# Filler products moved between the slots of attention and the stage behind it in a one-layer decoder block

## The chip, the cores and the metric

The kernel runs on one core of a Trainium2 chip. The metric is the device time of one execution in microseconds (us). Before the change it is 1077.14 us, the median of three runs (1077.08 to 1079.26). The product of two float32 matrices is made of three products of split operands throughout: each operand is written as a high part (rounded to fp32r) plus a low part (the rest), and high by high, high by low and low by high are summed in PSUM. So each "product" below is one TensorE instruction of a triple.

## The reference, cut to what matters

One layer over 1024 tokens of width 1024, all float32:

```
h   = rms_norm(x, norm1_g);  z = h @ w_in                  # 1024 x 2304
mix = [pool mixer | short gated conv | conformer conv | differential attention]   # 4 x 256 columns
x   = x + mix @ w_out
h2  = rms_norm(x, norm2_g)
x   = x + (silu(h2 @ w_gate) * (h2 @ w_up)) @ w_down       # inner width 2816

attention, 4 heads, each with two score maps m = 0, 1 of depth 32:
  p_m = softmax(q_m k_m^T / sqrt(32) + relative bias, causal)
  o   = rms_norm((p_0 - lam * p_1) @ v) * (1 - lam_init)
```

## The kernel before, in words

**Stages.** First come the norm and the input projection with the three convolution mixers (to about 244 us), then attention (244 to 400 us), then the end of the output projection and the second norm (to about 450 us), then the gated feed-forward part, which makes up the rest and which the change does not touch.

**Attention** is cut into 16 units u = 4p + h (p: a pair of 128-token query tiles, h: a head). `unit` writes down, for each of the two query tiles i and the two maps m, the scores (TensorE, line 673), the bias and the row minimum (VectorE, lines 680 and 681) and the exponential (ScalarE, line 684). VectorE then joins the two maps (lines 686 to 688). For each of the p + 1 key blocks kb, TensorE transposes the joined map (line 699), ScalarE and VectorE split it into high and low parts (lines 703 and 704), and TensorE multiplies it with v (line 708), first with the high parts, then with the low ones. Every second unit ends with a transposition of the output (line 720, tile `oT`). `prep_q` makes the stacked queries of the next heads (`kst`, made by ScalarE and by POOL or VectorE, transposed at line 510).

**Fillers.** Beside that runs a queue `fillq` of TensorE work that attention does not wait for. In order it holds the 288 products of the output projection of the three other mixers (`gen_partial`: 16 tiles of 18 products, numbered 1 to 288 here, tile `fm`), then for each finished p the 25 steps of `out_attn`, and at the last p two times four steps of `norm2`. `fill1` takes the next n steps from the queue, where n is the next entry of FQ:

```
def fill1(ins, n=None):
    for _ in range(next(slots, 0) if n is None else n):
        ...
                    with tc.issue_after(ins.ins):
                        f()
```

`issue_after(ins)` lets the filler be issued on TensorE only behind `ins`, the attention instruction that was just written. The call is the gate, its place in the text is the rank. One `fm` bank in PSUM serves all tiles of `gen_partial`, so the first product of a tile waits until the bank of the tile before has been read out (line 632 on ScalarE or line 635 on VectorE). The weights of `w_out` come in two column halves c, each of three pairs of tiles (a high one by line 120 or 122, a low one by POOL at line 134). Products 1 to 144 use half 0, products 145 to 288 half 1, which is loaded into the same six buffers.

**The slots.** FQ has 180 entries, one for each call of `fill1` without a count. A unit has two slots at `prep_q` (units 4, 8 and 12 at their start for their own second half of heads; units 2, 6 and 10 for the next p), four at the scores, two for each key block (after the transposes, and after the product with the high parts), one at its end, and one after `oT` in odd units. The units begin at slots 0, 7, 15, 24, 32, 43, 53, 64, 74, 87, 99, 112, 124, 139, 153 and 166. In both kernels the queue is empty at slot 179.

**The stage behind attention.** A second queue holds 48 products of the first gate and up columns, and later 48 more. `run_fill` writes a generator's steps and takes `ns[n]` fillers behind its step n + 1. FL and FB use up 27 of the first 48, while the last `out_attn` runs. FA stands behind the four transposition steps of `norm2(PO[2])`, where 21 are left. FC stands behind those of `norm2(PO[3])`, with the second 48. `drain` writes down what is left, without gates.

**Order.** The text is not the order of execution. The framework plans it (`schedule_with_timeline_sim=True`): on each engine it takes the instruction written first among those that its own simulated clock holds ready, and the engine then runs this fixed order. An instruction that is held back by its inputs in that plan is overtaken by later ones.

Of the kernel before, what the change touches and what calls it, by code (L numbers as in the profile page):

```python
# [33 lines left out]
PQ0 = 2  # L34
PQ1 = 0
PO = [0, 1, 2, 3]
FQ = [13, 0, 1, 0, 4, 0, 0, 0, 0, 0, 5, 6, 1, 4, 0, 0, 0, 0, 6, 1, 2, 5, 1, 0, 3, 0, 0, 2, 0, 4, 0, 1, 6, 0, 1, 9, 0, 1, 0, 0, 3, 5, 0, 3, 1, 4, 0, 3, 2, 0, 0, 4, 0, 5, 2, 0, 1, 1, 0, 2, 0, 0, 0, 0, 1, 0, 2, 0, 0, 0, 7, 0, 0, 0, 0, 0, 0, 5, 5, 5, 5, 0, 2, 7, 2, 0, 0, 3, 3, 3, 3, 0, 1, 2, 0, 2, 2, 0, 0, 1, 1, 10, 0, 3, 1, 0, 3, 4, 0, 1, 0, 0, 12, 4, 2, 1, 3, 2, 8, 1, 3, 0, 2, 6, 2, 0, 1, 5, 4, 2, 2, 3, 2, 1, 2, 0, 1, 0, 0, 2, 1, 0, 0, 4, 0, 0, 1, 0, 3, 0, 1, 4, 0, 0, 0, 2, 0, 14, 6, 0, 1, 12, 2, 1, 9, 3, 0, 0, 0, 3, 1, 2, 13, 10, 0, 3, 0, 4, 0, 20]
FL = [9, 1, 2, 0, 0, 2]
N2F = 0
FA = [0, 5, 19, 17]  # L40
FB = [11, 1, 0, 0, 0, 0, 0, 0, 0, 0, 0, 0, 0, 0, 1, 0, 0, 0, 0, 0, 0, 0, 0, 0, 0]
FC = [11, 5, 5, 2]
X1 = [1, 1, 1, 1, 1, 1, 1, 1, 0, 1, 1, 1, 0, 1, 1, 1]
SPE = [2, 2, 1, 0, 0, 1, 0, 1, 1, 0, 0, 0, 0, 1, 2, 2, 0, 2, 0, 2, 0, 0, 0, 0, 0, 1, 0, 0, 0, 0, 0, 0, 1, 0, 0, 0, 2, 1, 0, 1, 2, 2, 2, 2, 2, 2, 0, 0]
WOE = [0, 0, 1, 0, 1, 0, 0, 0]
# [21 lines left out]
def tile_hybrid(ctx, tc, x, norm1_g, w_in, pool_w, pool_scale, sconv_w, conf_w, conf_b, ln_g, ln_b,  # L67
# [570 lines left out]

    slots = iter(FQ)

# [101 lines left out]
    def out_attn(p, ps_o=None):  # L742
        ps_o = ps_o or ps_fm
        if p == PO[0]:
            wo[3] = [load_wo(3, c) for c in range(2)]
        ps = ps_tp()

        def tr():
            for k in range(2):
                for i in range(2):  # L750
                    ins = T.transpose(ps[:, k * 256 + i * P:k * 256 + (i + 1) * P], qn[p][:, i, k * P:(k + 1) * P], ident)
            return ins

        yield tr
        mh = misc.tile([P, 2, 256], R, name="mh", tag="mh")
        ml = misc.tile([P, 2, 256], R, name="ml", tag="ml")
        psv = ps.rearrange("p (a b) -> p a b", a=2)
        A.activation(mh, psv, AF.Copy, scale=subg)
        V.scalar_tensor_tensor(ml, psv, subg, mh.bitcast(F), op0=ALU.mult, op1=ALU.subtract)
        for i in range(2):  # L760
            t = 2 * p + i
            for c in range(2):
                po = ps_o()
                W = wo[3][c]
                for k in range(2):
                    yield from mms(po, (mh[:, k, i * P:(i + 1) * P], ml[:, k, i * P:(i + 1) * P]), (W[0][:, k], W[1][:, k]),
                                   k == 0, k == 1)
                sl = slice(c * 512, (c + 1) * 512)
                if X1B[PO.index(p)]:
                    tm = stp.tile([P, 512], F, name="tm", tag="st")  # L770
                    A.copy(tm, po)
                    G.tensor_tensor(x1[t][:, sl], x1[t][:, sl], tm, op=ALU.add)
                else:
                    V.tensor_tensor(x1[t][:, sl], x1[t][:, sl], po, op=ALU.add)

    def drain():
        while fillq:
            f = next(fillq[0], None)
            if f is None:
                fillq.pop(0)  # L780
            else:
                f()
# [10 lines left out]
    def norm2(p, ps_n=None):  # L793
        if p == PO[0]:
            W0.append(wgu(w_gate, 0))
            h2["hi"] = [m8.tile([P, 4, 512], R, name="h2a", tag="m8"), m8.tile([P, 4, 512], R, name="h2b", tag="m8")]
            h2["lo"] = [m8.tile([P, 4, 512], R, name="h2c", tag="m8")]
            h2["lo"] += [spp.tile([P, 512], R, name=f"h2lo{k}", tag="sp") for k in range(4)]
        if p == PO[2]:
            h2["k1"] = [ktp.tile([P, 2, 4, 512], R, name=f"h2k{k}", tag="KT") for k in range(2)]  # L800
        c0 = (p % 2) * 256
        xn = norm_xn([x1[2 * p], x1[2 * p + 1]], lambda: stp.tile([P, 1024], F, name="xn2", tag="st"), split=NX[PO.index(p)])

        def diff(kt, src):
            o, d = (tf[i][:, kt % 4, c0:c0 + 256] for i in (1, 2))
            if kt < 4:
                hi, lo = (a[:, c0:c0 + 256].bitcast(F) for a in h2rhs(0, kt))
                V.scalar_tensor_tensor(o, src, g2[:, kt:kt + 1], hi, op0=ALU.mult, op1=ALU.subtract)
                V.tensor_tensor(o, o, lo, op=ALU.subtract)
            else:  # L810
                V.scalar_tensor_tensor(d, src, g2[:, kt:kt + 1], o, op0=ALU.mult, op1=ALU.subtract)

        yield from norm_T(xn, g2, lambda kt: tuple(a[:, c0:c0 + 256] for a in h2rhs(p // 2, kt)),
                          ps_n or ps_tp, 2, diff if p // 2 == 1 else None)

    def wgu(w, f0, wpool=None, tag="w", stage=None):
        return wsplit(w[:, f0:f0 + P].rearrange("(k p) c -> p k c", p=P), (8,), wpool, tag, stage)
# [28 lines left out]
    def gu_items(k, W):  # L846
        for s in range(2):
            for kt in range(8):
                yield from mms(pgu[k][s], (W[s][0][:, kt], W[s][1][:, kt]), h2rhs(PO[0] // 2, kt), kt == 0, kt == 7)

    def run_fill(gen, ns):
        for n, f in enumerate(gen):
            ins = f()
            fill1(ins, ns[n % len(ns)])

    def alt(*ts):
        n = [0]

        def nxt():
            n[0] += 1  # L860
            return ts[n[0] % len(ts)]() if callable(ts[0]) else ts[n[0] % len(ts)]

        return nxt
# [4 lines left out]
    if N2F:  # L868
        run_fill(norm2(PO[2], alt(ps_tp, ps_fm)), FA)
    run_fill(out_attn(PO[3], alt(*pgu[1])), FB)  # L870
# [7 lines left out]
    if not N2F:  # L878
        run_fill(norm2(PO[2], alt(ps_tp, ps_fm)), FA)
    W1 = [wgu(w, P, _B(ap4, b), t, ap4.tile([P, 1024], F, name="st1", tag="at", bufs=ATB))  # L880
          for w, b, t in ((w_gate, PT1, "pt1"), (w_up, PT0, "pt0"))]
    fillq.append(gu_items(1, W1))
    run_fill(norm2(PO[3], alt(ps_tp, ps_fm)), FC)
    drain()
# [301 lines left out]
```

## Time and profile before

| | us |
|---|---|
| median of three runs | 1077.14 |
| the profiled execution | 1077.97 |
| its span, first to last instruction | 1076.2 |
| TensorE busy | 1045.2 (97%) |
| VectorE busy | 736.7 (68%) |
| ScalarE busy | 439.8 (41%) |
| GpSimd (POOL) busy | 222.9 (21%) |
| mean granted TensorE clock | 0.995 |

How to read it: the engines are PE (TensorE, with PEld for its weight loads), DVE (VectorE), ACT (ScalarE), POOL (GpSimd) and SP (the queue that issues transfers). L673 is line 673 of the kernel. A matrix product is shown with its latency, so the busy time of PE overlaps itself in a dense stretch. The distance between the starts of two products tells what one costs there.

### The profile page before, as it was taken

What the parts mean: (1) busy time and instruction counts of PE and PEld (TensorE: products, weight loads), DVE (VectorE), ACT (ScalarE), POOL (GpSimd) and SP (SyncE); (2) the same over time, 40 slices, a digit from 0 to 9 for tenths busy, and PEclk for the clock granted to TensorE, in tenths of its full rate; (3) what the DMA queues carried; (4) which work ended last, traced back from release to release, by engine and by line L of the source; (5) the groups of instructions that cost most, each with busy time, mean ns of one, the idle gap of its engine ahead of it and who ended that gap; (6) DMA issues with size and microseconds to landing.
All of it is one profiled execution on the core that took longest, in us unless ns stands there. A gap on an engine that the chain in (4) does not pass through costs nothing.

```text
span 1076.2 us, 13520 instructions
## 1 busy us (share of the span) xinstructions
PE 1045.2 (97%) x5203; PEld 875.9 (81%) x5203; DVE 736.7 (68%) x1127; ACT 439.8 (41%) x710; POOL 222.9 (21%) x202
## 2 busy tenths in 40 slices
PE   7999999998989989899999999999999999999998
PEld 6878879996778877787888888888888878888886
DVE  5599995648899966886676566567657656755541
ACT  5512124536786766432432333333233343433320
POOL 5137124665675643000000000000000000000000
PEclk8999999999999999999999999999999999999999
DMA  8131110111021130022353454445255286866721
GB/s 217 49 98 40 59 40 21 40 41 40 30 79 41 49 93 25 9 61 88 117 207 101 162 206 148 131 171 200 94 176 205 101 311 230 295 196 212 233 103 40
DMA packets 89664, 128.04 MB, mean 119 GB/s; under 512 B 17112, under 2 KB 57600, under 8 KB 87040
## 3 DMA queue, kind: packets, MB, share of 16 engines
q1 hardware_dynamic: 89600, 127.18, 35.9%
q8 instruction: 41, 0.67, 0.3%
q14 instruction: 23, 0.19, 0.1%
HBM read 94.13 MB, written 33.04 MB: 118 GB/s over the span
## 4 chain that ended last, share of the span: by engine, by line
PE 81%; DVE 8%; DMA 4%; ACT 3%; issue 1%; POOL 1%; SPq 1%; ACTq 0%; POOLq 0%; DVEq 0%
PE sb L139 11%; PE sb L138 11%; PE sb L140 11%; PE mm L139 6%; PE mm L140 6%; PE mm L138 6%; PE dx L140 3%; PE dx L139 3%; PE dx L138 3%; PE dy L138 3%; PE dy L140 3%; PE dy L139 3%; PE fm L604 1%; PE fm L606 1%; PE fm L605 1%
## 5 line engine op out<-in xcount | busy, mean ns | idle before, releaser
L139 PE MATMUL sb<-T,rhi 128*128 128x512 f32 x320 | 124.6, 389 | 0.0
L140 PE MATMUL sb<-T,rlo 128*128 128x512 f32 x320 | 124.5, 389 | 0.0
L138 PE MATMUL sb<-T,rhi 128*128 128x512 f32 x320 | 124.5, 389 | 0.0
L911 DVE TENSOR_TENSOR dq<-ds,dq 128x2048 fp32r<-128x2048 f32 x35 | 79.9, 2290 | 57.0 <-ACT dq L910 53.9
L910 ACT CAST dq<-ds 128x2048 fp32r<-128x2048 f32 x35 | 66.6, 1912 | 105.8 <-PE dy L140 34.5
L134 POOL TENSOR_TENSOR wlo<-st,whi 128x1024 fp32r<-128x1024 f32 (+2 forms) x30 | 73.9, 2468 | 109.7 <-ACT whi L120 98.5
L138 PE MATMUL mm<-hT,whi 128*128 128x512 f32 (+1 forms) x224 | 79.6, 367 | 2.6 <-ACT whi L120 2.0
L139 PE MATMUL mm<-hT,whi 128*128 128x512 f32 (+1 forms) x224 | 81.4, 367 | 0.6 <-DVE hT L200 0.5
L140 PE MATMUL mm<-hT,wlo 128*128 128x512 f32 (+1 forms) x224 | 80.6, 363 | 0.3 <-POOL wlo L134 0.3
L317 DVE SCALAR_TENSOR_TENSOR t<-u,cw,t 128x1023 f32<-128x1023 f32 (+28 forms) x58 | 71.4, 1266 | 0.7
L140 PEld LDWEIGHTS sb<-T,rlo 128*128 128x128 f32 x320 | 60.1, 188 | 12.5
L138 PEld LDWEIGHTS sb<-T,rhi 128*128 128x128 f32 x320 | 60.1, 188 | 12.5
L139 PEld LDWEIGHTS sb<-T,rhi 128*128 128x128 f32 x320 | 60.1, 188 | 12.4
L910 ACT CAST rhi<-st 128x1024 fp32r<-128x1024 f32 x28 | 29.5, 1054 | 98.4 <-PE sb L139 49.5
L139 PE MATMUL dx<-dq 128*128 128x512 f32 x160 | 62.5, 390 | 1.3 <-DVE dq L911 1.3
L140 PE MATMUL dx<-dq 128*128 128x512 f32 x160 | 62.3, 390 | 0.0
L138 PE MATMUL dx<-dq 128*128 128x512 f32 x160 | 61.3, 390 | 0.0
L684 ACT ACTIVATE pt<-sc,mx 128x128 f32<-128x128 f32 (+7 forms) x64 | 47.6, 747 | 18.2 <-DVE mx L681 18.1
L138 PE MATMUL mm<-whi,hT 128*128 128x256 f32 x192 | 55.0, 290 | 0.0
L139 PE MATMUL mm<-wlo,hT 128*128 128x256 f32 x192 | 54.7, 286 | 0.0
L140 PE MATMUL mm<-whi,hT 128*128 128x256 f32 x192 | 54.5, 285 | 0.0
L1031 DVE TENSOR_TENSOR tp<-tp,sb 128x512 f32<-128x512 f32 x30 | 20.5, 684 | 45.2 <-PE sb L140 45.2
(342 smaller groups left out, 2698.3 us busy)
## 6 DMA issues: line engine op xcount, KB each, us to landing
ds<-dL SPq DMA_DIRECT2D x35, 512.0 KB, 4.1
wd<-in_w_down_dram SPq DMA_DIRECT2D x10, 1024.0 KB, 5.2
dT<-wd SPq DMA_DIRECT2D x10, 1024.0 KB, 6.0
dL<-afs SPq DMA_DIRECT2D x10, 1024.0 KB, 3.9
ds<-dT SPq DMA_DIRECT2D x20, 512.0 KB, 6.0
st<-in_w_in_dram SPq DMA_DIRECT2D x18, 512.0 KB, 3.8
st<-in_w_gate_dram SPq DMA_DIRECT2D x15, 512.0 KB, 4.2
st<-in_w_up_dram SPq DMA_DIRECT2D x15, 512.0 KB, 3.7
```

The lines of the kernel that those rows point to most:

```text
L134: G.tensor_tensor(lo[:, nv:], st[:, nv:], hi[:, nv:].bitcast(F), op=ALU.subtract)
L138: T.matmul(ps, lhsT=L[0], rhs=Rr[0], start=first, stop=False, skip_group_check=more)
L139: T.matmul(ps, lhsT=L[0], rhs=Rr[1], start=False, stop=False, skip_group_check=more)
L140: return T.matmul(ps, lhsT=L[1], rhs=Rr[0], start=False, stop=last, skip_group_check=more)
L317: V.scalar_tensor_tensor((z if s == 30 else acc)[:, s:], u[:, :S - s], w[:, 30 - s:31 - s], acc[:, s:], op0=ALU.mult, op1=ALU.add)
L604: yield lambda: T.matmul(ps, lhsT=L[0], rhs=Rr[0], start=first, stop=False)
L605: yield lambda: T.matmul(ps, lhsT=L[0], rhs=Rr[1], start=False, stop=False)
L606: yield lambda: T.matmul(ps, lhsT=L[1], rhs=Rr[0], start=False, stop=last)
L684: A.activation(pts[m][:, 0:w], sc[:, 0:w], AF.Exp, bias=mx, scale=-1.0, accum_out=lt[:, h, m, i:i + 1])
L910: A.copy(hi, src)
L911: (eng or V).tensor_tensor(lo, src, hi.bitcast(F), op=ALU.subtract)
L1031: V.tensor_tensor(s, s, ps, op=ALU.add)
```

## The change

Three lists of quotas are changed and nothing else. The sum of FQ stays 387.

```
-FQ = [13, 0, 1, 0, 4, 0, 0, 0, 0, 0, 5, 6, 1, 4, 0, 0, 0, 0, 6, 1, 2, 5, 1, 0, 3, 0, 0, 2, 0, 4, 0, 1, 6, 0, 1, 9, 0, 1, 0, 0, 3, 5, 0, 3, 1, 4, 0, 3, 2, 0, 0, 4, 0, 5, 2, 0, 1, 1, 0, 2, 0, 0, 0, 0, 1, 0, 2, 0, 0, 0, 7, 0, 0, 0, 0, 0, 0, 5, 5, 5, 5, 0, 2, 7, 2, 0, 0, 3, 3, 3, 3, 0, 1, 2, 0, 2, 2, 0, 0, 1, 1, 10, 0, 3, 1, 0, 3, 4, 0, 1, 0, 0, 12, 4, 2, 1, 3, 2, 8, 1, 3, 0, 2, 6, 2, 0, 1, 5, 4, 2, 2, 3, 2, 1, 2, 0, 1, 0, 0, 2, 1, 0, 0, 4, 0, 0, 1, 0, 3, 0, 1, 4, 0, 0, 0, 2, 0, 14, 6, 0, 1, 12, 2, 1, 9, 3, 0, 0, 0, 3, 1, 2, 13, 10, 0, 3, 0, 4, 0, 20]
+FQ = [16, 0, 1, 3, 4, 0, 0, 0, 3, 0, 7, 6, 1, 4, 0, 0, 0, 0, 6, 1, 2, 3, 1, 0, 3, 0, 0, 3, 0, 4, 0, 1, 2, 0, 1, 5, 0, 1, 0, 0, 3, 3, 0, 3, 1, 4, 0, 3, 2, 0, 0, 4, 0, 10, 2, 0, 1, 1, 0, 2, 0, 0, 0, 0, 1, 0, 2, 0, 0, 0, 5, 0, 0, 0, 5, 0, 0, 5, 4, 4, 4, 0, 7, 3, 2, 1, 0, 2, 2, 2, 2, 0, 1, 2, 0, 2, 2, 0, 0, 1, 1, 7, 0, 3, 1, 0, 3, 4, 0, 1, 0, 0, 12, 4, 2, 1, 3, 2, 8, 1, 3, 0, 2, 6, 2, 0, 1, 5, 4, 2, 2, 3, 2, 1, 2, 0, 1, 0, 0, 2, 1, 0, 0, 4, 0, 0, 1, 0, 3, 0, 1, 4, 0, 0, 0, 2, 0, 14, 8, 0, 1, 12, 7, 1, 6, 2, 0, 0, 0, 3, 1, 2, 10, 10, 0, 3, 0, 4, 0, 20]
-FA = [0, 5, 19, 17]
+FA = [0, 11, 19, 23]
-FC = [11, 5, 5, 2]
+FC = [6, 4, 3, 2]
```

Slot by slot, with the number of fillers by which the changed queue is ahead after it ("lead"):

| slots (unit) | change | lead after |
|---|---|---|
| 0, 3 (u0), 8, 10 (u1) | +3, +3, +3, +2 | 11 |
| 21 (u2), 27 (u3) | -2, +1 | 10 |
| 32, 35, 41 (u4) | -4, -4, -2 | 0 |
| 53 (u6, first prep step) | +5 | 5 |
| 70 (u7) | -2 | 3 |
| 74 (u8, first prep step) | +5 | 8 |
| 78, 79, 80 (u8) | -1 each | 5 |
| 82, 83, 85 (u8) | +5, -4, +1 | 7 |
| 87 to 90 (u9) | -1 each | 3 |
| 101 (u10) | -3 | 0 |
| 158, 162, 164, 165 (u14) | +2, +5, -3, -1 | 3 |
| 172 (u15) | -3 | 0 |

In FA, 21 fillers are left: before, 5 and 16 are taken behind the second and the third step; now 11 and 10. In FC, 23 of 48 are gated before, 15 now.

## Rows read from the trace of the kernel before

**Rows 1.** The page: TensorE's busy line, and the chain that ended last, by engine.

```profile
PE 1045.2 (97%) x5203; PEld 875.9 (81%) x5203; DVE 736.7 (68%) x1127; ACT 439.8 (41%) x710; POOL 222.9 (21%) x202
...
PE 81%; DVE 8%; DMA 4%; ACT 3%; issue 1%; POOL 1%; SPq 1%; ACTq 0%; POOLq 0%; DVEq 0%
```

**Rows 2.** Stretches: us; busy PE, PEld, DVE, ACT, POOL (instructions); clock, DMA, GB/s.

```profile
244.00:261.00 17.00, 14.16 (x70) 10.49 (x69) 14.60 (x51) 9.12 (x34) 9.74 (x9) 1.00 0.15 48
261.00:284.00 23.00, 22.43 (x124) 17.98 (x123) 20.39 (x68) 16.81 (x47) 17.30 (x21) 1.00 0.11 35
284.00:298.00 14.00, 12.61 (x77) 10.46 (x76) 12.30 (x42) 11.02 (x30) 7.64 (x11) 1.00 0.10 33
298.00:306.00 8.00, 8.00 (x46) 6.88 (x46) 7.51 (x20) 6.01 (x14) 4.14 (x5) 1.00 0.16 54
306.00:318.00 12.00, 9.39 (x57) 7.52 (x56) 11.89 (x27) 10.34 (x23) 10.00 (x8) 1.00 0.21 67
318.00:332.00 14.00, 12.96 (x75) 10.99 (x76) 13.17 (x37) 9.51 (x22) 8.54 (x7) 1.00 0.26 89
332.00:374.00 42.00, 42.00 (x245) 36.34 (x243) 39.24 (x83) 29.74 (x59) 27.71 (x32) 1.00 0.14 45
...
434.00:446.00 12.00, 9.21 (x49) 6.97 (x48) 11.14 (x27) 7.11 (x15) 0.89 (x2) 0.98 0.00 0
```

**Rows 3.** TensorE in time order, 246 to 257 us: start, duration, [idle before <-releaser].

```profile
251.02 0.73 PE L673 MATMUL sc<-KT,QT 128*128 128x256 f32 x2 [0.69 <-ACT pt L684]
...
256.34 0.44 PE L699 MATMUL tp<-ident,pt 128*128 128x128 f32 x2 [0.51 <-DVE pt L688]
```

**Rows 4.** TensorE and VectorE in time order about slots 32 to 35.

```profile
272.21 0.48 PE L606 MATMUL fm<-whi,sp 128*128 128x512 f32 x1
...
275.07 0.39 PE L606 MATMUL fm<-whi,sp 128*128 128x512 f32 x1
...
275.96 0.27 PE L699 MATMUL tp<-ident,pt 128*128 128x128 f32 x1
...
274.35 1.16 DVE L688 SCALAR_TENSOR_TENSOR pt<-pt,cf 128x512 f32<-128x512 f32 x1
```

**Rows 5.** TensorE in time order: four waits, and the filler behind the last.

```profile
292.05 0.66 PE L510 MATMUL tp<-ident,kst 128*128 128x128 f32 x4 [1.14 <-POOL kst L506]
...
314.01 0.74 PE L708 MATMUL av<-at,VV 128*128 128x256 f32 x4 [1.19 <-DVE at L704]
...
324.73 0.50 PE L605 MATMUL fm<-wlo,sp 128*128 128x512 f32 x1 [0.93 <-POOL wlo L134]
...
387.79 0.51 PE L708 MATMUL av<-at,VV 128*128 128x256 f32 x2 [1.27 <-DVE at L704]
...
388.38 0.48 PE L604 MATMUL fm<-whi,mh 128*128 128x512 f32 x1
```

**Rows 6.** TensorE 303 to 309 us, and the ScalarE copy that the transposes at L720 read.

```profile
303.05 0.39 PE L604 MATMUL fm<-whi,sp 128*128 128x512 f32 x1
...
305.34 0.39 PE L605 MATMUL fm<-wlo,sp 128*128 128x512 f32 x1
305.57 0.60 PE L720 MATMUL tp<-ident,oT 128*128 128x128 f32 x4
306.01 0.60 PE L510 MATMUL tp<-ident,kst 128*128 128x128 f32 x4
...
308.39 0.66 PE L510 MATMUL tp<-ident,kst 128*128 128x128 f32 x4 [1.08 <-POOL kst L506]
...
302.84 0.59 ACT L120 COPY oT<-av 128x512 f32<-128x512 f32 x1 [0.29 <-PE av L708]
```

**Rows 7.** POOL: the addition for the last tile of half 0, and the third low part of half 1.

```profile
315.06 1.30 POOL L633 TENSOR_TENSOR x<-x,xr 128x512 f32<-128x512 f32 x1
...
321.71 2.96 POOL L134 TENSOR_TENSOR wlo<-st,whi 128x1024 fp32r<-128x1024 f32 x1 [0.91 <-ACT whi L120]
```

**Rows 8.** TensorE behind attention: the third step of `norm2(PO[2])`.

```profile
437.78 0.63 PE L190 MATMUL fm<-ident,xn 128*128 128x128 f32 x4 [1.19 <-DVE tf L808]
```

## The prediction

> **What bounds the kernel now.** I read the page first: TensorE is busy for 1045.2 of 1076.2 us, and 81% of the chain that ended last is TensorE's [rows 1]. So the time is TensorE's work plus what TensorE waits. The change leaves the work alone: the same products run, and by slot 179 the filler queue is empty in both kernels. Only waits can change, and only from 244 us (the first slot) to about 446 us.
>
> Next I read the stretches of that part [rows 2]. The reader is to compare the columns PE and DVE in each line, because the bound changes hands. From 244 to 261 us neither engine is full (PE idles 17 - 14.16 = 2.84 us, DVE 2.40). From 261 to 284 PE is nearly full (22.43 of 23) and DVE has 2.61 us of room. From 284 to 298 PE idles 1.39 and DVE 1.70. From 298 to 332 DVE is the full one: 7.51 + 11.89 + 13.17 = 32.57 of 34 us. From 332 to 374 PE is busy for all of its 42 us. From 434 to 446, behind attention, it is DVE again (11.14 of 12).
>
> Last I read TensorE in order of time for the waits themselves [rows 3, 5, 6, 8]. The price of a filler comes from the eleven products that start from 303.05 to 305.34 [rows 6]: ten steps in 2.29 us, so 0.229 us each. The fillers that start from 272.21 to 275.07, thirteen of them, give 2.86 / 12 = 0.238 [rows 4]. I use 0.23.
>
> **The change part by part.** A filler moved is worth 0.23 us where it goes into a wait, if the place it leaves does not become a wait in its turn. So each part has two questions.
>
> *Slots 0 to 10 (+11) against slots 21 to 41 (-11).* Eleven fillers are 2.53 us. The waits that they can reach are 0.69 us before the scores at 251.02 and 0.51 before the transposes at 256.34 [rows 3]: 1.2 us. The other 1.3 us lengthen the first stretch. Behind it, 2.53 us leave a stretch in which PE is nearly full. If PE gives all of it back the net is -1.2; if nothing comes back it is +1.3. There is one place where it can't all come back: of the thirteen fillers at 272.21, eight go (slots 32 and 35), but the transposes behind them, at 275.96, need a joined map that VectorE ends at 274.35 + 1.16 = 275.51 [rows 4]. They can come 0.45 us earlier at most by that map, against 8 x 0.23 = 1.84. What saves the rest is that VectorE itself has 2.61 us of room there and gets its scores earlier. The nearest row is the one of the stretch, PE 22.43 of 23, so I stay near its end and take -0.9.
>
> *Slot 53 (+5), paid by slots 70 (-2) and 101 (-3).* The five go behind the first preparation step of unit 6 and in front of the wait of 1.14 us for POOL's `kst` at 292.05 [rows 5]; 5 x 0.23 = 1.15 fill it. Cover for the cost: that wait is POOL's, so no one is held up. Product 109 opens a new `fm` tile in the middle of the five and waits for the bank, which may leave some of the gap open. What it is worth is decided where the five are missing. The three of slot 101 run in the stretch in which PE never waits: 3 x 0.23 = 0.69, and DVE has 42 - 39.24 = 2.76 us of room there [rows 2]. I take -0.7, bounds 0 and -0.7. The two of slot 70 are missing in 298 to 306, where PE is busy 8.00 of 8 and DVE has 0.49 us of room: 0.46 at most, I take -0.4, bounds 0 and -0.46.
>
> *Slots 74 to 90 (+5 at 74, +5 at 82, +1 at 85, -11 at 78 to 80, 83 and 87 to 90).* Nothing is carried out of this part. It fills the waits of 1.08 us at 308.39 [rows 6] and 1.19 at 314.01 [rows 5], and takes the fillers from places that lie some us later in the same stretch, in which VectorE has 0.11 us of room (306 to 318) and 0.83 (318 to 332) [rows 2]. I count it as 0; its bounds are -2.3, the two waits gone, and the +2.5 of the rival below. One thing in it isn't bound by VectorE. Product 158 waits 0.93 us at 324.73 for the third low part of half 1 [rows 5], which POOL makes from 321.71 on [rows 7]. That weight needs a staging buffer which the last tile of half 0 gives back when POOL has added it, at 315.06 + 1.30 [rows 7]. With the lead of 5 to 8, product 144 comes behind the first transposes of unit 8 instead of the second, and the load starts earlier. I take -0.5, bounds 0 and -0.93.
>
> *Slots 158 to 172, FA and FC.* The wait of 1.27 us at 387.79 [rows 5] stands behind fillers whose gates had long been open: 316 steps had been written by the transposes of unit 14's third block, and the filler that runs next, at 388.38 [rows 5], is only the 302nd, counted along the trace. They weren't late for want of quota, so more quota does not bring them. In FA, six more fillers go in front of the 1.19 us before 437.78 [rows 8] and six fewer behind it, in front of the next norm's transposes, while VectorE is busy 11.14 of 12 us [rows 2]: a wait that changes its place. FC reorders products in the stretch that follows. Together 0; bounds -1.3 (one such wait gone) and +1.3 (one more).
>
> *Sum:* -0.9 - 0.7 - 0.4 - 0.5 = -2.5 us. The profiled execution took 1077.97, 1.77 above its span and 0.83 above the median, so it would come to 1075.5; from the median, 1077.14 - 2.5 = **1074.6 us**.
>
> **The rivals.**
>
> *Every new filler fills its wait.* For it: each large increase stands in front of a wait: 0.69 + 0.51 [rows 3], 1.14 + 1.19 + 1.27 [rows 5], 1.08 [rows 6], 5.88 us in all. Against it: VectorE's lines from 298 to 332 [rows 2]. Time: 1077.14 - 5.9 = 1071.2.
>
> *VectorE sets the time.* If its order of work is the bound from 261 to 332 already, PE's waits only change places, and what stays is part of the -0.7 from the stretch where PE is full. For it: 32.57 of 34 us. Against it: PE at 22.43 of 23 before that. Time: about 1076.7. The Trainium skill, in Perfetto Trace Analysis, section Identifying the Most-Contended Engine, says that time is won on the engine of highest occupancy, and that TensorE is to be judged by its weight loads rather than by its matmul time. By that rule the trace sides with this rival from 298 to 332 (VectorE 96%, weight loads 6.88 + 7.52 + 10.99 = 25.39 of 34 us, 75%) and with the forecast from 332 to 374 (weight loads 36.34 of 42, 87%).
>
> *The gate at slot 74 starves TensorE (slower).* Before, slot 74 is empty, and products 126 to 137 belong to the scores of unit 8 (up to slot 79). Those scores had run early, so the gates were open, and the products from 303.05 to 305.34 filled TensorE while the output of unit 7 was copied out [rows 6]. Now 126 to 130 may not run before the first preparation step of unit 8 (306.01), and all later ones queue behind them. If the plan leaves the transposes of `oT` and of that step where they are, TensorE has nothing from 303.05 to 305.57 and does the eleven products afterwards: +2.5 us, 1079.6. It decides on whether `oT` moves up. The copy that it reads ends at 302.84 + 0.59 = 303.43 [rows 6], so on the chip it can come 2.1 us earlier, and then nothing is lost. The plan's own clock may not see that.
>
> *The change hardly does what it says.* The plan ranks by its own idea of what is ready, and fillers that weren't ready at their slots stay where they were. Time: 1077.1.
>
> **How the numbers follow.** What a measurement of this kernel can tell from no change is about 0.2%, 2.15 us: faster is below 1074.99, slower above 1079.29. Forecast 0.38, with a range of its own of 1073.2 to 1076.2, three quarters of it faster (0.28) and the rest the same (0.10). All waits filled 0.20, faster. VectorE 0.16 and hardly a change 0.06, the same. Starved at slot 74 0.20, slower. So faster 0.48, same 0.32, slower 0.20. For the range, the lower end goes past the 1071.2 of the first rival by a part of the bound of the last weights' wait (0.7), to 1070.5; the upper end past the 1079.6 of the slower one by a part of the 1.3 of the first part, to 1080.0.
>
> **What would show it.** Right: PE's idle time from 244 to 261 falls by about 1.2 us, the waits at 292 and 325 all but go, eleven fillers between 284 and 306 run earlier, and unit 10's block behind slot 101 starts about 2 us earlier than 333.8. VectorE's part right: waits of about a microsecond before `at` or `pt` remain between 298 and 332. Starved: PE idle in front of `oT` of unit 7, none of which the trace of before has. Wrong altogether: the fillers' numbers stand at the same attention instructions as before, or the part behind attention moves by more than 1.3 us against attention's end.

## The result, and the profile after

The changed kernel takes 1101.38 us (median of 4 runs, 1097.14 to 1103.73) against 1077.29 beside it: ratio 1.0219, interval 1.0202 to 1.0237. It is slower by 24.1 us, where 2.5 us less were forecast. Its profiled execution took 1097.14, with a span of 1095.4; it is the shortest of the four, so its trace shows 19.2 of the 24.1 us, and the other three ran at a lower mean granted clock (0.989 to 0.994 against 0.995).

The page of the kernel after: the lines that answer to [rows 1].

```profile
PE 1054.1 (96%) x5203; PEld 879.6 (80%) x5203; DVE 735.9 (67%) x1127; ACT 440.1 (40%) x710; POOL 222.5 (20%) x202
...
PE 80%; DVE 8%; DMA 4%; ACT 4%; issue 1%; SPq 1%; POOL 1%; ACTq 0%; POOLq 0%; DVEq 0%
```

The same counts on every engine: the work is the same. A cut at the end of attention's part says where the time goes. The first fence is the kernel before, the second the kernel after (columns as in [rows 2]); the first lines of the second answer to [rows 2].

```profile
244.00:443.00 199.00, 184.26 (x1002) 149.63 (x1000) 167.37 (x413) 134.55 (x301) 111.28 (x109) 1.00 0.15 48
443.00:1076.00 633.00, 625.36 (x2752) 516.27 (x2752) 391.17 (x475) 214.04 (x241) 4.78 (x2) 1.00 0.47 161
```

```profile
244.00:261.00 17.00, 14.81 (x69) 10.97 (x68) 14.23 (x51) 9.57 (x35) 10.82 (x12) 1.00 0.15 49
261.00:284.00 23.00, 19.34 (x95) 14.90 (x94) 17.15 (x62) 14.51 (x41) 13.56 (x17) 0.93 0.10 34
...
298.00:306.00 8.00, 6.20 (x33) 5.15 (x32) 6.46 (x20) 3.99 (x11) 2.35 (x4) 0.90 0.09 34
...
244.00:463.00 219.00, 191.65 (x997) 151.87 (x995) 166.16 (x415) 134.57 (x301) 108.05 (x109) 0.98 0.14 44
463.00:1095.00 632.00, 625.12 (x2752) 516.27 (x2751) 390.59 (x473) 213.73 (x241) 6.56 (x2) 1.00 0.48 162
```

Read the last line of each: behind attention nothing is lost. All of it lies in the 200 us before, where PE idles 219 - 191.65 = 27.35 us instead of 14.74, and VectorE, which needs 166 or 167 us there, does the same work in 20 us more. Idle time is 12.6 of these 20 us. The other 7.4 stand in PE's busy time, 191.65 against 184.26 us for nearly the same instructions (997 and 1002): a product that overlaps no other counts with its whole latency (0.39 us, against the 0.23 between two starts), and the mean clock is 0.98. What each of the two takes isn't separated here. From 261 to 284, where PE was nearly full, it now idles 3.66 us.

TensorE of the kernel after, in order of time (start, duration, [idle before <-releaser]):

```profile
250.05 0.65 PE L673 MATMUL sc<-KT,QT 128*128 128x256 f32 x2
...
256.47 0.44 PE L699 MATMUL tp<-ident,pt 128*128 128x128 f32 x2 [0.54 <-DVE pt L688]
...
258.68 0.46 PE L604 MATMUL fm<-whi,sp 128*128 128x512 f32 x1
...
262.64 0.39 PE L606 MATMUL fm<-whi,sp 128*128 128x512 f32 x1
262.88 0.60 PE L720 MATMUL tp<-ident,oT 128*128 128x128 f32 x4
...
265.25 0.89 PE L673 MATMUL sc<-KT,QT 128*128 128x384 f32 x2 [1.10 <-ACT pt L684]
...
278.04 0.44 PE L673 MATMUL sc<-KT,QT 128*128 128x384 f32 x1 [0.85 <-ACT pt L684]
...
294.75 0.66 PE L510 MATMUL tp<-ident,kst 128*128 128x128 f32 x4 [0.17 <-POOL kst L506]
...
303.27 0.62 PE L673 MATMUL sc<-KT,QT 128*128 128x512 f32 x2 [1.64 <-ACT pt L684]
...
306.13 0.63 PE L605 MATMUL fm<-wlo,sp 128*128 128x512 f32 x1
306.56 0.63 PE L606 MATMUL fm<-whi,sp 128*128 128x512 f32 x1
306.98 0.63 PE L604 MATMUL fm<-whi,sp 128*128 128x512 f32 x1
...
310.21 0.66 PE L720 MATMUL tp<-ident,oT 128*128 128x128 f32 x4 [0.67 <-ACT oT L120]
```

The waits that were to be filled are filled: that of 0.69 in front of a score [rows 3] is gone (250.05), and the 1.14 for `kst` [rows 5] are 0.17 (294.75). Of the 5.88 us that the first rival of the prediction adds up over six waits, 0.71 are left in this trace (0.54 and 0.17). But new ones stand in front of scores, at 265.25, 278.04 and 303.27. And from 258.68 on eighteen products run in one block in front of unit 1's `oT`, where six stood before.

The next table is worked out from the start times of the traces: how much later than before each unit's last product with v starts, in us. The columns are the kernel after and the experiments, which are numbered e1 to e13 in the next section. Ahead of the first units the profiled executions differ by -0.6 to +1.1 us of themselves (row of unit 1), which is to be taken off.

```
unit  (before)  after   e1    e2    e5    e7    e8    e9   e11   e12   e13
  1     259.1   -0.4   0.6   1.1   0.5  -0.4  -0.6   0.7   0.6   0.7   0.7
  3     269.8    4.0   4.5   1.1   5.0  -0.4  -0.6   0.7   0.5   4.3   4.5
  5     287.1    3.5   4.0   1.1   7.2   2.7   2.5   3.8   0.6   5.5   4.0
  7     302.6    6.7   7.3   2.2   7.8   3.5   3.4   4.5   0.5   6.2   7.6
  8     318.6    8.2  11.5   3.9   7.9   3.6   3.2   4.5   0.5   6.2  11.9
 10     340.9   10.6  16.1  13.2   7.9  11.0   7.6   4.5   0.9   6.2  12.0
 13     374.7   16.2  17.6  10.8   7.9   9.8  10.4   4.5   1.2   6.2  12.0
 15     400.6   21.7  22.1  15.3   8.9   8.0   9.4   4.6   5.8   7.3  13.0
```

### The profile page after: what moved, and what is told of

Same layout as the page of the kernel before. It is cut to its first block, busy times and chain, and to the rows that moved or that the text cites. A ratio compares the mean times of both kernels' runs of the same rounds, so it can differ in the third digit from the quotient of the medians.

```text
span 1095.4 us, 13536 instructions
## 1 busy us (share of the span) xinstructions
PE 1054.1 (96%) x5203; PEld 879.6 (80%) x5203; DVE 735.9 (67%) x1127; ACT 440.1 (40%) x710; POOL 222.5 (20%) x202
## 4 chain that ended last, share of the span: by engine, by line
PE 80%; DVE 8%; DMA 4%; ACT 4%; issue 1%; SPq 1%; POOL 1%; ACTq 0%; POOLq 0%; DVEq 0%
PE sb L139 11%; PE sb L138 11%; PE sb L140 11%; PE mm L139 6%; PE mm L140 6%; PE mm L138 6%; PE dx L140 3%; PE dx L139 3%; PE dx L138 3%; PE dy L138 3%; PE dy L139 2%; PE dy L140 2%; PE fm L604 2%; PE fm L605 2%; PE fm L606 1%
## 5 line engine op out<-in xcount | busy, mean ns | idle before, releaser
L120 ACT CAST whi<-st 128x1024 fp32r<-128x1024 f32 x28 | 29.4, 1050 | 53.9 <-PE mm L139 42.1
```

What stands on the lines that cost most here:

```text
L120: A.copy(dst, src)
```

## The experiments

Each time stands beside runs of the kernel before on the same chip, at 1077.1 to 1077.4 us.

**The four parts, each alone.** *e1: slots 0 to 41.*

```diff
-slots 0 3 8 10 21 27 32 35 41: 13 0 0 5 5 2 6 9 5
+slots 0 3 8 10 21 27 32 35 41: 16 3 3 7 3 3 2 5 3
```

> Only the early quotas are changed (slots 0 to 41, lead 11 falling back to 0). Theory of place: fillers that now stand in front of attention's instructions hold them up, and the loss ends where the lead ends. The last product with v of unit 4 was 4.6 us late in the changed kernel, so this one should take 1077.2 + 4.6 = about 1082, with the delay constant from unit 5 on. Theory of the plan: the order of all engines is drawn anew behind the first changed slot, and the loss comes from that order; then this part alone should give most of the 24 us, 1089 or more, and the delay should go on growing behind unit 4.

1099.07 us, ratio 1.0203 (1.0186 to 1.0220): +21.9. Theory of the plan.

*e2: slots 53 to 101.*

```diff
-slots 53 70 74 78 79 80 82 83 85 87-90 101: 5 7 0 5 5 5 2 7 0 3 each 10
+slots 53 70 74 78 79 80 82 83 85 87-90 101: 10 5 5 4 4 4 7 3 1 2 each 7
```

> Only the quotas of slots 53 to 101 are changed. Theory of place: the changed kernel lost 10.2 - 4.6 = 5.6 us between units 4 and 9, so about 1083, lost in front of unit 10. Theory of the plan: a loss that begins at unit 6 and grows to the end of attention, 1085 to 1092.

1090.16, ratio 1.0118 (1.0103 to 1.0133): +13.0. Theory of the plan, by its range.

*e3: slots 158 to 172.*

```diff
-slots 158 162 164 165 172: 6 2 9 3 13
+slots 158 162 164 165 172: 8 7 6 2 10
```

> Only the quotas of slots 158 to 172 are changed. Theory of place: the changed kernel lost 21.7 - 16.2 = 5.5 us from unit 13 to unit 15, so about 1082.5. Theory of the plan: little is left behind these slots to be drawn anew, so 1077 to 1079.

1081.31, ratio 1.0038 (1.0024 to 1.0053): +4.2, nearer to the theory of place. The loss comes in unit 15: it ends 6.6 us late (unit 14 only 0.5), and 2.5 are given back behind it. Counted in the two programs, TensorE's 480 attention instructions stand here in the same order as before; the steps of the queue stand elsewhere between them. Behind unit 15 stand waits on VectorE of 1.3 us, where the kernel before has none above 0.43 from 400 to 420 us:

```profile
410.15 0.51 PE L604 MATMUL fm<-whi,mh 128*128 128x512 f32 x1 [1.32 <-DVE x L774]
...
415.52 0.63 PE L720 MATMUL tp<-ident,oT 128*128 128x128 f32 x4 [1.26 <-DVE h2lo L200]
417.50 1.06 PE L190 MATMUL tp<-ident,xn 128*128 128x128 f32 x8 [1.36 <-DVE h2lo L200]
```

*e4: FA and FC.*

```diff
-FA = [0, 5, 19, 17]
+FA = [0, 11, 19, 23]
-FC = [11, 5, 5, 2]
+FC = [6, 4, 3, 2]
```

> Only FA and FC are changed. The changed kernel lost no more behind attention than in it (the step at 443.40 came 19.4 us late, the last product with v 21.7), so both theories expect 1076 to 1079; above 1080 the stage behind attention would be a cause of its own.

1079.32, ratio 1.0019 (1.0010 to 1.0028): +2.2, a little above the range of both theories. Its one trace doesn't say where: 1.6 us longer, of which 0.9 stand ahead of the first transposes of attention.

The parts lose 41.3 us alone and 24.1 together: not prices of places that add up. In e1 the delay grows from 7.3 us at unit 7 to 22.1 at unit 15, though no quota behind slot 41 differs. So the early part changes something that lasts. The programs show what: 201 of TensorE's 480 attention instructions stand in e1 where they stand in the order before, and scores 46 to 95 stand up to 21 transposes and products earlier among the others.

**The order held.** All scores (and so, mostly, all of attention) are tied to the place that they have in the kernel before (the edit is shortened; the comment stands for it):

```diff
+                    with held():   # issue_after the transpose, product with v or prep step
+                                   # that this score follows in the kernel before
                     ins = T.matmul(sc[:, c0:c0 + n], ...
```

*e5: with the quotas of e1.*

> The quotas of the first experiment (slots 0 to 41 changed, all others as before) and, beside them, an order: each score matmul may be placed on TensorE only behind that transpose or product with v behind which it stands in the kernel before (with the quotas of before this order changes nothing in the program). TensorE's attention instructions then stand in 457 of 480 places as in the kernel before, and from the 32nd of the 96 scores on all of them; without the order it is 201. The fillers stand as the changed quotas say. Theory of the plan (scores that slip ahead of the transposes cost the time, to the end): 1077 to 1083 us, most of the 21.9 us of the first experiment come back. Theory of the place (the fillers added in front of attention, and taken from between its scores, cost where they stand): 1095 to 1100, as without the order.

1086.24, ratio 1.0083 (1.0068 to 1.0098): +9.0 in place of +21.9. Between the two theories, nearer to that of the plan: 12.9 us come from the order, and 9.0 remain. The table shows what an equal order does: from unit 7 to unit 13 the delay stands at 7.8 to 7.9.

*e6: with all of the change.*

> All of the change, and the same order for the scores. It can keep a score from coming too early, not from coming too late: 312 of 480 attention instructions of TensorE stand as before (267 without the order), and the scores that are left elsewhere stand later, much as in the second experiment. Theory of the plan: the part of the loss that early scores make is gone and the part of late ones is left: 1084 to 1092 us, near the second experiment's 1090.2 and well under 1101. Theory of the place: 1098 to 1103.

1098.75, ratio 1.0196 (1.0176 to 1.0215). The theory of the plan missed by 7 us: nearly nothing comes back. The hold can't bring a late score forward. Counted in the programs, many scores that stand up to 11 places early in the changed kernel stand up to 13 places late in e6, where e2 has them: one redrawn order takes the place of another. The time is near the sum of the two parts, 9.0 (e5) + 13.0 (e2) = 22.0 against 21.5.

**One product fewer.** *e7: the order free.*

```diff
-slot 32: 6
+slot 32: 5
```

> The kernel before with one product fewer in one slot: 5 in place of 6 at slot 32; the one left over is taken in the last slot. Worked out from the program, 316 of 480 attention instructions of TensorE keep their place, and scores 51 to 94 stand up to 9 transposes and products too early. Theory of the plan: a loss like that of the second experiment (323 of 480, 13 us), 1082 to 1092 us, out of one product of 0.47 us. Theory of the place: 1076.5 to 1077.8, no change that can be told.

1088.79, ratio 1.0108 (1.0092 to 1.0124): +11.6 from one product of 0.23 us (the 0.47 of the expectation are two). Theory of the plan.

*e8: the same quota, the order held as in e5.*

> One product fewer at slot 32 as in the run before it, and the order for the scores: 432 of 480 attention instructions stand as before, all scores but 6 in their places. Theory of the plan: 1076.5 to 1080 us, the loss of the kernel without the order is gone. Theory of the place: as without the order, 1076.5 to 1077.8; so this run counts only beside the one before it.

1089.74, ratio 1.0120 (1.0104 to 1.0137). A miss: with nearly all scores back among the transposes as before, nothing is won. So here the scores that stand early cost nothing on balance. One part of what is left belongs to a score that still stands elsewhere: at unit 5 both traces lose 3.1 us at one step. There score 23 (counted from 0) stands behind eleven products in front of which it stands in the kernel before. The larger part doesn't: from unit 8 to unit 13 the delay of e8 grows from 3.2 to 10.4 us, and by the programs the six scores out of place belong to units 5, 7, 14 and 15. What stands elsewhere in units 8 to 13 are mostly products of the queue, beside a few transposes and products with v. What these cost wasn't tried alone.

**One score, no quota.** *e9.*

```diff
+SN, FN = [23], 89
...
+                    with tc.issue_after(frec[FN].ins) if nsc[0] in SN else ExitStack():
                     ins = T.matmul(sc[:, c0:c0 + n], ...
```

> No quota is changed: the kernel before, with a single one of its scores (the 24th, counted from 0: number 23) placed by an order behind products 79 to 89, the block of eleven products in front of which it stands in the kernel before. It is the place that it has in the runs with one product fewer. All other scores but two keep their place among the transposes and products (470 of 480 instructions), and from number 32 on all stand as before. In the three runs where this score stood behind the block, the transposes of its unit came 2 to 3.2 us later than the instructions ahead of them. Theory of the block (a score that isn't ready at its turn is passed over for the whole block of products, and the transposes behind it wait): 1079.2 to 1081, and the delay stands at about 3 us from 286 us on and grows no more. Theory that the changed quotas themselves cost, by the place of the products: 1076.5 to 1077.8, for no product is moved.

1081.73, ratio 1.0045 (1.0032 to 1.0057): +4.5, a little over what was expected, with all quotas as before. TensorE and VectorE of the kernel before about this score, in order of time:

```profile
279.25 0.50 PE L673 MATMUL sc<-KT,QT 128*128 128x512 f32 x1
...
279.91 0.46 PE L605 MATMUL fm<-wlo,sp 128*128 128x512 f32 x1
...
282.29 0.39 PE L606 MATMUL fm<-whi,sp 128*128 128x512 f32 x1
...
283.71 0.77 PE L699 MATMUL tp<-ident,pt 128*128 128x128 f32 x5 [0.20 <-DVE pt L688]
...
280.08 0.61 DVE L680 TENSOR_REDUCE fmx<-sc 128x1 f32<-128x256 f32 x2
```

The same of the kernel with the one score held (its lines stand 1 to 4 further on):

```profile
280.58 0.44 PE L606 MATMUL fm<-wlo,sp 128*128 128x512 f32 x1
...
282.93 0.39 PE L607 MATMUL fm<-whi,sp 128*128 128x512 f32 x1
283.16 0.39 PE L676 MATMUL sc<-KT,QT 128*128 128x512 f32 x1
...
285.59 1.00 PE L676 MATMUL sc<-KT,QT 128*128 128x512 f32 x2 [0.86 <-ACT pt L688]
...
287.27 0.55 PE L703 MATMUL tp<-ident,pt 128*128 128x128 f32 x3 [0.68 <-DVE pt L692]
...
283.58 0.62 DVE L684 TENSOR_REDUCE fmx<-sc 128x1 f32<-128x256 f32 x2 [2.75 <-PE sc L676]
```

Before, the score runs at 279.25, the eleven products after it keep TensorE busy to 282.5, and beside them VectorE and ScalarE do that tile's minimum, exponential and join. Held, the products come first and VectorE sits idle for 2.75 us. When the score is out, TensorE has used up the work that was its cover, and waits for the exponential and the join. The transposes come at 287.27 instead of 283.71, 3.56 us later (0.66 of it were there ahead of the score). By unit 7 the delay is 4.5, and it stands there to the end, since all behind is as before.

Why the plan puts it there can only be read from the two orders. In e7 the block is reached one product, 0.23 us, earlier, and it seems that the plan doesn't hold the score ready by then. It takes a product, which was written earlier than the score, and at every next step there is another such product, until the block is through. Held behind product 82 or 84 instead of 89 (counted from 0, as FN counts), this score comes to the same place, behind the whole block, in the program. That is how 0.23 us would become the length of a block; the plan's own clock wasn't read.

**Two quotas, the order kept.** *e10.*

```diff
-slots 29 32: 4 6
+slots 29 32: 5 5
```

> Slot 32 has 5 products in place of 6, as in the run with one product fewer, and slot 29 has 5 in place of 4: the product is moved three slots forward. TensorE's 480 attention instructions all stand as before, and one product stands on the other side of score 19. Theory of the block: 1076.5 to 1078, no change, though the same quota is changed that cost 11.6 us. Theory that slot 32 wants its 6th product: 1086 to 1090, as in the run with one product fewer.

1077.04, ratio 0.9999 (0.9990 to 1.0008): no change. Slot 32 has the 5 of e7; the order is as before, and so is the time. Beside e9 this is the plainest pair: here a product moves by three slots and the order stays, and that costs nothing; there the order changes without a quota, and that costs 4.5 us. It doesn't hold for every quota: e3 keeps the order of attention too and costs 4.2 us.

**Another pair of scores.** *e11: the edit of e9 with other numbers.*

```diff
+SN, FN = [58, 59], 171
```

> No quota is changed: the kernel before with scores 58 and 59 (one tile's pair, 337 us into the run before) placed by an order behind products 162 to 172, the block of eleven that they stand in front of. Here the rest of the order doesn't come back by itself: 362 of 480 attention instructions stand as before, and scores up to number 95 stand up to 13 transposes and products later. Theory of the block: 2 to 3.5 us later at the first transposes behind the block, and more behind that, for later scores stand late too: 1081 to 1092 us. Theory that the block is paid for only once, with no more lost behind it: 1079 to 1080.8. Theory of the quotas by place: 1076.5 to 1077.8.

1080.03, ratio 1.0037 (1.0023 to 1.0051): +2.8, the time of "paid once", but not for that reason. At the first units behind the block (10 and 11) the delay is 0.9 and 0.5, with 0.6 there from the start; it comes at units 14 and 15, 50 us later. The redrawn order has scores late from unit 11 on, and which of them costs the time isn't shown. That the block itself costs next to nothing here and 3 us in e9 fits a block being dear only where TensorE has nothing else in hand behind it; two blocks don't prove it.

**The added products alone.** *e12.*

```diff
-slots 0 3 8 10 40 41 43 45: 13 0 0 5 3 5 3 4
+slots 0 3 8 10 40 41 43 45: 16 3 3 7 0 1 0 3
```

> The change's eleven additions at slots 0, 3, 8 and 10, paid for at slots 40, 41, 43 and 45 instead (3, 4, 3 and 1 products fewer), with the order for the scores of the held runs. Score 23 keeps its place in front of its block of products this time, and 460 of 480 attention instructions stand as before, from score 32 on all. So what is left is the eleven products themselves in front of the scores of the first units. In the held run of the early slots the delay was 4.5 to 5 us ahead of score 23, and 9.0 us in all. Theory that the additions hold up the scores they stand in front of and that this is not given back: 1081 to 1082.5. Theory that the 4.5 us of score 23 are all that costs, and the products added in front are given back where they were taken: 1077 to 1078.5. The term that was forecast for these slots, a gain of 0.9 us: 1076.3.

1083.38, ratio 1.0056 (1.0042 to 1.0070): +6.0, more than any of the three. Unit 3 is 3.6 us late by the table (4.3 - 0.7), and taking the same eleven products away later gives nothing of it back for good: the delay falls to 2.9 in unit 4, is 5.5 in unit 5 and stands at 6.2 from unit 7 to unit 13. Four scores stand one to three places late here, so the 6.0 aren't the products alone.

**Only the second half held.** *e13: the quotas of e1; the hold is given in words.*

```diff
+scores below 46: free; from 46 on: held as in e5
```

> The early slots of the change once more, with the order for the scores from number 46 on alone. The first 46 scores stand exactly as in the first experiment (free order), and those from 60 on as in the kernel before; there the first experiment has them up to 21 transposes and products earlier. Theory that scores which stand early cost (they block TensorE's queue at the wait for one of the two score tiles): the delay stays near the 7 to 8 us that it has at unit 7 in the first experiment, and the time is 1084 to 1088 us. Theory that early scores cost nothing, as in the pair with one product fewer, and the loss is made by scores 21 to 35: 1095 to 1099.5, as in the first experiment.

1089.94, ratio 1.0123 (1.0106 to 1.0140): +12.7, between the two, nearer to the first. So the 21.9 us of the early slots are 9.0 (e5), 12.7 - 9.0 = 3.7 between the held and the free order of scores 21 to 35, and 21.9 - 12.7 = 9.2 of the order from score 46 on. In that second half (units 9 to 15), in order: the kernel before, e1, e13 (whose lines stand 11 or 12 further on); columns as in [rows 2].

```profile
318.00:401.00 83.00, 79.58 (x457) 67.42 (x457) 71.14 (x151) 57.47 (x112) 50.39 (x48) 1.00 0.19 60
```

```profile
330.00:423.00 93.00, 82.97 (x447) 68.39 (x445) 67.69 (x140) 54.60 (x108) 45.95 (x46) 0.94 0.15 46
```

```profile
330.00:414.00 84.00, 78.65 (x454) 66.39 (x453) 71.21 (x149) 56.72 (x111) 46.63 (x46) 1.00 0.17 51
```

And VectorE's costliest waits there, of the same three (line, operation | busy, mean ns | idle before, and what ended it):

```profile
L704 DVE TENSOR_TENSOR at<-tp,at 128x512 fp32r<-128x512 f32 (+1 forms) x26 | 16.6, 640 | 6.3 <-ACT at L703 6.3
L687 DVE SCALAR_TENSOR_TENSOR cf<-lt,nlam,cf 128x1 f32<-128x1 f32 x12 | 4.2, 352 | 0.5 <-ACT pt L684 0.4
```

```profile
L704 DVE TENSOR_TENSOR at<-tp,at 128x512 fp32r<-128x512 f32 (+1 forms) x25 | 16.1, 647 | 11.6 <-ACT at L703 11.4
...
L687 DVE SCALAR_TENSOR_TENSOR cf<-lt,nlam,cf 128x1 f32<-128x1 f32 x11 | 4.1, 375 | 6.4 <-ACT pt L684 6.4
```

```profile
L716 DVE TENSOR_TENSOR at<-tp,at 128x512 fp32r<-128x512 f32 (+1 forms) x25 | 16.0, 645 | 6.0 <-ACT at L715 6.0
L698 DVE SCALAR_TENSOR_TENSOR cf<-lt,nlam,cf 128x1 f32<-128x1 f32 x12 | 4.5, 374 | 0.6 <-ACT pt L695 0.5
```

With the order free VectorE waits 5.3 us more in front of `at` and 5.9 in front of `cf`; with the order held both are back, though the first 46 scores stand as in e1. The quotas are the same in the second and the third.

## Why the prediction was wrong

**The step that failed** is the rule on which every term stands: "A filler moved is worth 0.23 us where it goes into a wait, if the place it leaves does not become a wait in its turn." It takes the order of the other instructions as given. The order is what the change redraws: of 480 attention instructions 267 keep their place, and what the places of scores cost is larger than all the waits that were priced. e9 shows it with no quota changed (4.5 us), e5 for 12.9 of the 21.9 us of e1, and e13 for 9.2 of these. The rule fails in a second place as well. Where attention's order stays or nearly stays, moved products still cost more than 0.23 us each in e3 (4.2 us, all 480 places kept) and e12 (6.0 us for 2.53 us of products, 460 kept). There a product's own length doesn't tell its price.

*Bounds of the kernel.* Right: the same work, and the change of time lies between 244 us and the end of attention. Not all of it is waits: 7.4 us are longer busy time. Reading which engine is full in a stretch was right too, but it was read as a property of the stretch; VectorE's share of 32.57 in 34 us [rows 2] hangs on scores that come in time (in the kernel after, 6.46 of 8 us from 298 to 306).

*Slots 0 to 10 against 21 to 41, -0.9, bounds -1.2 and +1.3.* The 0.69 us were filled, the 0.51 were not (0.54 at 256.47). The upper bound was too low in kind: it let the products' own 2.53 us be lost at most. In e12, which pays for them at other slots, the cost is 6.0 us with nearly all of attention in its order, and in e5 9.0 with score 23 late as well. Eighteen products stand in front of `oT` of unit 1 instead of six, so the scores of the next units come late, and "VectorE gets its scores earlier" is the wrong way round.

*Slots 53 to 101, -0.7, -0.4 and -0.5.* In the whole change the wait for `kst` went as priced (1.14 to 0.17), and that for the weights [rows 5] is gone; the part alone fills less of the first (0.82 left) and costs 13.0. Its order is redrawn too (323 of 480 places kept), but how much of the 13.0 that makes wasn't separated.

*Slots 158 to 172, FA and FC, 0 with 1.3 on both sides.* +4.2 and +2.2: outside. The wait of 1.27 us was read rightly, more quota alone doesn't fill it (1.24 left in e3). But attention's order is the same in both, so a redrawn order of attention can't be the reason. In e3 steps of the queue stand in front of unit 15's last transposes and products with v, and new waits of 1.3 us stand behind it. For e4 no cause is shown.

*The rivals.* The condition of the first, every new filler in its wait, nearly came true (0.71 of 5.88 us left), and its time is the farthest off. The starved gate at slot 74 shows as 0.67 us in front of unit 7's `oT` (310.21), a quarter of its price. "The change hardly does what it says" looked at the right part, the plan, and drew the opposite from it. No rival let the loss go on where no quota changes.

**Open.** How the 24.1 us of the whole change split isn't settled: its order isn't any of the parts' orders, and holding it gave 2.6 us back, because the hold puts scores late instead. The trace holds 19.2 of them. Early scores cost 9.2 us in e1 (up to 21 places) and nothing in e7 against e8 (up to 9); what makes the difference wasn't tried. The growth of e8 in units 8 to 13 has no cause shown. No order was tried that brings a late score forward.

## What to carry to other kernels

Where a planner writes the order at build time, a knob that moves work is a knob on the whole order behind it: compare the orders of the two programs before pricing any wait, and price first the instructions that feed the other engines. A block of filler was cover for the chain that was started before it; started behind it, the same chain had none (e9). Tying the critical instructions to their old places is the experiment that tells the cost of the order from the cost of the quotas, and neither is to be taken as nothing.

## What was not expected

Besides the waits, TensorE also ran slower. Behind the wait of 1.64 us at 303.27 the products start 0.43 us apart (306.13, 306.56, 306.98) instead of 0.23, and the stretch from 298 to 306 shows a granted clock of 0.90: part of it ran at the lower level, 1.2 GHz. In e1's second half the clock was 0.94 on the mean, where before and in e13 it was 1.00. Worked out from these rows as an estimate, up to 93 x 0.06 = 5.6 of the 9.2 us between e1 and e13 can be the lower clock, which came with the free order, and not the waits themselves.
